# Hybrid decoder block: the first norm from squares of the transposed input, row blocks of the second product group prepared one ahead, and modulation rows summed by fp32r products

## The chip, the cores and the metric

The kernel runs on one NeuronCore of one Trainium2 chip. The metric is the device time of one execution in microseconds (us). The engines are named as in the profile: PE (TensorE, the matrix products; its weight loads are PEld), DVE (VectorE), ACT (ScalarE), POOL (GpSimd) and SP (SyncE, which only issues transfers here). Each runs its own instructions in order and waits on the others by semaphores.

## The reference, cut to what matters

The block takes x (1024 tokens by 1024 channels, float32), a conditioning vector c and weights. What the change touches is the beginning, and the rows of the modulation that are needed later:

```
silu_c = silu(c)
mod = silu_c @ w_ada + b_ada              # 6 * 1024 columns
shift1, scale1, gate1, shift2, scale2, gate2 = split(mod, 6)
h = rms_norm(x, norm1_w) * (1 + scale1) + shift1
proj = h @ w_in                           # v, q, k, a_lr, sv, r, g_a, su, g_b ...
...                                       # gated linear attention, spatial gating, merge, w_out
x = x + gate1 * y
h2 = rms_norm(x, norm2_w) * (1 + scale2) + shift2
...                                       # PEER: top-16 of 16384 experts for 8 heads, gathers
x = x + gate2 * y2
out = rms_norm(x, final_norm_w)
```

rms_norm divides each token by the root of the mean of its squared channels (plus 1e-6).

## The kernel before

**Precision.** A float32 product is split: an operand is rounded to fp32r (its high part, written by ACT), DVE subtracts that from the operand (its low part, also fp32r), and three fp32r products stand for one. In the first group the even row blocks of weights are multiplied whole, in plain fp32, and only the odd ones are split.

**Halves.** The tokens are worked in two halves of 512. For the first half the first two groups of products (the two halves of the columns of v, `w_inp[G_V0]` and `w_inp[G_V1]`) are written out by hand in `first_groups`, because the modulation, the norm and the weights arrive at the same time as they are needed. Every instruction there goes through `put`, which chains it behind the instruction before it on its engine, so that the order in the source is the order on each engine. (The profile shows all of these at line 1088, the line of `put`; they are told apart by their tiles.) After that the order is the planner's, within the edges that `issue_after` gives.

**First group, rounds q = 0 to 3.** The contraction runs over 8 row blocks k of 128 channels. `xts[k]` is x transposed, 128 channels by 512 tokens; `wts[k]` is a row block of weights. Round q handles the blocks ka = 2q (by `whole`: 4 fp32 products) and kb = 2q+1 (by `products`: 12 fp32r products into the same 4 PSUM banks `mm`), and meanwhile forms the scale columns of the next round: `channel_sums` multiplies 8 row blocks of `w_ada` by silu(c) and adds them up (`add`: the first on ACT, the others on DVE, tile `adc`), `close` sums over the partitions by products with a column of ones on PE (tile `aux`), and `store_scale` writes `mod` and `scol` on DVE. The next round's `scaled` on ACT multiplies `xts` by `scol`, in place, and needs that. The first group is computed without the norm, and its result is scaled by `rstd` per token when it leaves PSUM (`evac0`, tile `vt`). The shift is added much later (`shift_rows`, `shift_sum`, `shift_add`).

**The norm.** x itself, tokens on partitions, is read into four tiles `xb` (512 KB each). ACT squares each and sums along the row (`squares(0)` in round 2, `squares(2)` in round 3). `norm` scales the four sums on DVE and takes the power -0.5 on POOL; `norm_spread` writes `dg`, a diagonal matrix of rstd, on DVE; `norm_rows` multiplies it by ones on PE and copies the result to `rrow` on ACT. In round 3 the order on PE is: 4 whole products of block 6, `norm_rows`, the 12 products of block 7, `close` for the shift columns.

**Second group, k = 0 to 7.** Here the normed and shifted input is needed: `turn(k)` (DVE) multiplies `xts[k]` by `rrow` (and by `scol` for odd k), `split_h(k)` writes `hTh` (ACT) and `hTl` (DVE), `high` and `low` split the weights (`wh` on ACT, `wl` on DVE), then come 12 products and two small ones for the decay rank (`alpha`). In each step k everything of block k stands just before its products. DVE also sums the second half of the shift columns, two rows in each of the steps 0 to 3; `close` stands inside step 3, and `store_shift(nps, 1)` after it. After the group come `decay(0)` and `decay(1)`, and `shift_rows` may start behind the group's last DVE instruction (`hlast[1]`).

**Modulation rows.** The other four parts of the modulation are made during later groups of the first half, by `ada_row`: DVE sums 8 tiles of 128 by 1024 (tile `adacc`), and two fp32 products with a column of ones, each giving 1 by 512, sum over the partitions (line 1174).

**Pools.** `v4` has 4 buffers of 128 by 1024, `b4` has 8, `aux` has 2 PSUM banks.

Of the kernel before, what the change touches and what calls it, by code (L numbers as in the profile page):

```python
# [80 lines left out]
def block_kernel(ctx: ExitStack, tc: tile.TileContext, x, xT, cT, w_asc, w_ash, w_ada, b_ada, b_adaT, n1T, w_inp, w_alr,  # L81
# [27 lines left out]
    nc.vector.tensor_scalar(ident, jp, 0.0, None, op0=OP.is_equal)  # L109
    nc.vector.tensor_scalar(ltri, jp, 0.0, None, op0=OP.is_gt)  # L110
    nc.vector.memset(ones, 1.0)
    nc.vector.memset(mhalf, -0.5)
    for i in range(5):
        nc.vector.memset(bit5[:, i:i + 1], 1 << i)
# [905 lines left out]
    class Queue:  # L1020
# [4 lines left out]
        def add(self, g):  # L1025
            self.gens.append(g)
# [27 lines left out]
    with ExitStack() as pa:  # L1054
# [109 lines left out]
        def ada_row(c, r):  # L1164
            for acc in ada_acc(c):
                yield
            for _ in range(2):
                yield
            row_ = t4("adarow")
            nc.scalar.dma_start(row_[0:1], b_ada[:, c * D:(c + 1) * D])  # L1170
            for n in range(2):
                sl = slice(n * 512, (n + 1) * 512)
                ps = auxt([1, 512])
                nc.tensor.matmul(ps, ones[:, 0:1], acc[:, sl], start=True, stop=True)
                nc.vector.tensor_tensor(row_[0:1, sl], row_[0:1, sl], ps, op=OP.add)
            if r == 1:
                nrow = t4("nrow")
                nc.scalar.dma_start(nrow[0:1], n2_w)
                nc.vector.scalar_tensor_tensor(row_[0:1], row_[0:1], 1.0, nrow[0:1], op0=OP.add, op1=OP.mult)
            nc.scalar.dma_start(rows_d[r:r + 1, :], row_[0:1])  # L1180
            yield
# [28 lines left out]
                    xts.append(xt[:, kk])  # L1210
            return xts

        hlast = []

        def h_split(k):
            xt = xts[k]
# [7 lines left out]
        def first_groups(evac0, evac1, aps, finish_alpha, decay):  # L1224
# [97 lines left out]
            by_bank = [(n, i) for i in range(4) for n in range(3)]  # L1322

            rrow = t2("rrow")
            ss = sm_p.tile([P, BH], F32, name="ss")

            def squares(i0):
                for i in (i0, i0 + 1):
                    put("scalar", "activation", xb[i], xb[i], AF.Square, accum_out=ss[:, i:i + 1])

            def norm():
                rstd = sm_p.tile([P, BH], F32, name="rstd")
                rstd0.append(rstd)
                put("vector", "tensor_scalar", rstd, ss, 1.0 / D, EPS, op0=OP.mult, op1=OP.add)
                nc.gpsimd.tensor_tensor(rstd, rstd, mhalf[:, :BH], op=OP.pow)
# [24 lines left out]
            ps, prod, add, close = channel_sums(scs[0], [0, 1, 2, 3], 2 * P)  # L1360
            prod([0, 1, 2, 3])
            add(KD)
            close()
            store_scale(ps, 0)
            keep_warm(iota)
# [3 lines left out]
            scaled(hTh[:, 1], 1)  # L1369
            wl = low(wts[1], wh)  # L1370
            scaled_low(1)
            xb, shs = [], []
            for q in range(4):
                ka, kb = 2 * q, 2 * q + 1
                nps, _, add, close = channel_sums(scs[q + 1], [], 2 * P) if q < 3 else channel_sums(shs[0], [], 512)
                whole(pss, ka)
                if q == 3:
                    squares(2)
                add(1)
                if q < 3:  # L1380
                    nwh = high(wts[kb + 2])
                    if q == 2:
                        squares(0)
                    add(KD)
                    if q:
                        scaled_low(kb)
                    nwl = low(wts[kb + 2], nwh)
                else:
                    add(2)
                    norm()  # L1390
                    scaled_low(kb)
                    add(2)
                    norm_rows(norm_spread())
                    add(KD)
                cut = (8, 4, 4, 12)[q]
                order = by_bank if q == 3 else by_part
                products(pss, kb, wh, wl, order[:cut])
                close()
                products(pss, kb, wh, wl, order[cut:])
                if q == 0:  # L1400
                    scs.append(load_scale(3, b4))
                    load_x(6, 7)
                    load_w(6, 7)
                    for i in range(BH):
                        xb.append(v4.tile([P, D], F32, name="xb", tag="v4"))
                        put("sync", "dma_start", xb[i], x[i * P:(i + 1) * P, :])
                    put("sync", "dma_start", walr, w_alr)
                    load_w1(0)
                    shs.append(load_shift(0))
                    load_w1(1, 2)  # L1410
                if q == 2:
                    shs.append(load_shift(1))
                    load_w1(3, 4)
                    for dst, src_ in ((wal[:RANK], w_al), (wal[RANK:], w_al), (balt, b_alT), (keyst, keysT), (sgub, sgu_bT)):
                        put("sync", "dma_start", dst, src_)
                if q < 3:
                    store_scale(nps, q + 1)
                    scaled(xts[kb + 1], kb + 1)
                    scaled(hTh[:, kb + 2], kb + 2)
                    wh, wl = nwh, nwl  # L1420
                else:
                    for i in range(4):
                        evac0(i, pss[i])
                    turn(0)
                    nwh = high(w1[0])
                    store_shift(nps, 0)
                    nwl = low(w1[0], nwh)
            split_const(walr, walr2[:, :, :RANK], walr2[:, :, RANK:])
            keep0.extend(wts)
            nps, _, add, close = channel_sums(shs[1], [], 512)  # L1430
            pss1 = [mm.tile([P, 512], F32, name="mm", tag="mm") for _ in range(4)]
            for k in range(KD):
                if k:
                    turn(k)
                    nwh = high(w1[k])
                split_h(k)
                if k:
                    nwl = low(w1[k], nwh)
                if k + 5 < KD:
                    load_w1(k + 5)  # L1440
                if k == KD - 1:
                    alpha(aps, k, put)
                if k < 4:
                    add(2)
                order = by_bank if k in (0, KD - 1) else by_part
                products(pss1, k, nwh, nwl, order[:8])
                if k == 3:
                    close()
                products(pss1, k, nwh, nwl, order[8:])
                if k < KD - 1:  # L1450
                    alpha(aps, k, put)
                if k == 3:
                    store_shift(nps, 1)
                    split_const(wal, wal_h, wal_l)
# [3 lines left out]
                evac1(i, pss1[i])  # L1458
            decay(0)
            decay(1)  # L1460
            return tail["tensor"]

        S = []
# [39 lines left out]
        for hf in range(NHALF):  # L1503
# [70 lines left out]
            def shift_rows(k0):  # L1574
                if not shiftw:
                    shiftw.append(rp.tile([P, 512], F32, name="so", tag="so", bufs=2))
                for k in (k0, k0 + 1):
                    if k == 0:
                        with tc.issue_after(hlast[1]):
                            nc.vector.tensor_scalar(shiftw[0], keep0[0], mod[:, 0:1], None, op0=OP.mult)  # L1580
                    else:
                        nc.vector.scalar_tensor_tensor(shiftw[0], keep0[k], mod[:, k:k + 1], shiftw[0], op0=OP.mult, op1=OP.add)
# [496 lines left out]
```

## Time and profile before

| | |
|---|---|
| times of 3 runs | 1439.87, 1431.17, 1432.71 us; median 1432.71 |
| profiled execution, its own time | 1431.43 us |
| its span, first to last instruction | 1429.6 us (1.8 us lie around it) |
| PE busy | 1338.7 us, 94% of the span |
| DVE busy | 1085.0 us, 76% |
| ACT busy | 694.2 us, 49% |
| POOL busy | 291.5 us, 20% |
| DMA | 341.90 MB moved |
| mean granted PE clock | 0.972 |

The busy shares are means over the whole span. All but the four modulation rows of what the change touches lies in the first 92 us, and those rows lie between 187 and 284 us.

### The profile page before, as it was taken

How to read it: one execution, taken by the hardware profiler on the slowest of the kernel's cores; microseconds unless marked ns; L12 is line 12 of the kernel's file. 1: busy time of each engine (PE TensorE's matmuls, PEld its weight loads, DVE VectorE, ACT ScalarE, POOL GpSimd, SP SyncE). 2: the span in 40 equal slices, each digit the busy share in tenths (PEclk: the TensorE clock that was granted, in tenths of full speed). 3: DMA queues.
4: the chain of work that ended last, by engine and by line, in shares of the span. 5: the costliest groups of instructions: out<-in, count | busy, mean ns of one | idle time of the engine just before them, and what ended most of it. 6: DMA issues, size and time to landing. Idle time of an engine off the chain costs nothing. (4 is left out here: it accounts for less than half of the span.)

```text
span 1429.6 us, 19379 instructions
## 1 busy us (share of the span) xinstructions
PE 1338.7 (94%) x5952; PEld 1027.3 (72%) x5952; DVE 1085.0 (76%) x3094; ACT 694.2 (49%) x1561; POOL 291.5 (20%) x270
## 2 busy tenths in 40 slices
PE   9799999999999999988989999999998999789994
PEld 5578867788888887776867888877777876345552
DVE  5685569834468678999789887888798767898783
ACT  4364342333345465475344565655455545555542
POOL 0020001000000122341441142311111124453320
PEclk9899999999999999998999999999998999999997
DMA  9344446732257475777687799987687559998972
GB/s 361 131 155 134 137 152 203 252 97 83 94 177 264 160 276 176 274 236 243 205 285 255 244 357 333 332 305 243 234 294 284 197 171 382 349 386 340 369 292 104
DMA packets 111877, 341.90 MB, mean 239 GB/s; under 512 B 14505, under 2 KB 15785, under 8 KB 99602
## 3 DMA queue, kind: packets, MB, share of 16 engines
q0 software_dynamic: 31344, 163.85, 31.4%
q1 hardware_dynamic: 63072, 131.37, 27.0%
q10 hardware_dynamic: 17346, 45.34, 8.9%
q8 instruction: 48, 0.79, 0.2%
q14 instruction: 67, 0.55, 0.1%
HBM read 316.28 MB, written 24.23 MB: 238 GB/s over the span
## 5 line engine op out<-in xcount | busy, mean ns | idle before, releaser
L1497 ACT ACTIVATE wh<-wt 128x512 fp32r<-128x512 f32 x336 | 207.8, 627 | 280.8 <-PE mm L183 116.2
L1499 DVE TENSOR_TENSOR wl<-wt,wh 128x512 fp32r<-128x512 f32 x336 | 227.2, 689 | 109.2 <-ACT wh L1497 58.1
L182 PE MATMUL mm<-wh,hTh 128*128 128x512 f32 x624 | 246.0, 394 | 2.1 <-ACT wh L1497 2.1
L183 PE MATMUL mm<-wh,hTl 128*128 128x512 f32 x624 | 245.7, 394 | 0.0
L185 PE MATMUL mm<-wl,hTh 128*128 128x512 f32 x624 | 194.5, 395 | 2.2 <-DVE wl L1499 2.2
L182 PEld LDWEIGHTS mm<-wh,hTh 128*128 128x128 f32 x624 | 117.4, 188 | 28.8 <-ACT wh L1497 3.1
L185 PEld LDWEIGHTS mm<-wl,hTh 128*128 128x128 f32 x624 | 116.0, 188 | 29.6 <-DVE wl L1499 3.0
L526 POOL DMA_INDIRECT uv<-in_tab_dram,ix x74 | 80.6, 1089 | 274.7 <-ACT ix L558 170.9
L183 PEld LDWEIGHTS mm<-wh,hTl 128*128 128x128 f32 x624 | 117.2, 188 | 25.1 <-issue 0.9
L182 PE MATMUL mm<-hTh,wh 128*128 128x512 f32 x240 | 96.0, 400 | 0.0
L581 DVE SCALAR_TENSOR_TENSOR uv<-uv,hps 128x512 f32<-128x512 f32 x112 | 75.1, 684 | 26.7 <-DMA uv<-in_tab_dram,ix 16.0
L183 PE MATMUL mm<-hTl,wh 128*128 128x512 f32 x240 | 95.0, 396 | 0.0
L188 PE MATMUL mm<-wh,hTh 128*128 128x512 f32 x208 | 84.0, 410 | 4.7 <-DVE x L1886 2.1
L190 PE MATMUL mm<-wh,hTl 128*128 128x512 f32 x208 | 81.8, 393 | 0.0
L189 PE MATMUL mm<-wl,hTh 128*128 128x512 f32 x208 | 81.7, 393 | 0.0
L188 PE MATMUL mm<-hTh,wh 128*128 128x256 f32 (+1 forms) x208 | 71.2, 345 | 8.9 <-DVE q L1673 6.6
L185 PE MATMUL mm<-hTh,wl 128*128 128x512 f32 x240 | 72.3, 401 | 0.0
L189 PE MATMUL mm<-hTl,wh 128*128 128x256 f32 (+1 forms) x208 | 69.3, 335 | 3.1 <-DVE hTl L174 3.1
L753 POOL DMA_INDIRECT uvd<-in_down_dram,dix x32 | 38.2, 1193 | 163.9 <-DVE ts L360 47.2
L190 PE MATMUL mm<-hTh,wl 128*128 128x256 f32 (+1 forms) x208 | 68.2, 336 | 0.0
L619 DVE SCALAR_TENSOR_TENSOR vl<-uv,r,vh 128x512 fp32r<-128x512 f32 x82 | 59.6, 749 | 9.3 <-ACT vh L618 5.8
L607 PE MATMUL acc<-uv,W 128*128 128x512 f32 x132 | 63.4, 603 | 2.5 <-ACT W L596 1.9
(970 smaller groups left out, 2955.7 us busy)
## 6 DMA issues: line engine op xcount, KB each, us to landing
wt<-in_w_inp_dram SPq DMA_DIRECT2D x216, 256.0 KB
wt<-in_w_qp_dram SPq DMA_DIRECT2D x72, 256.0 KB
wada<-in_w_ada_dram SPq DMA_DIRECT2D x32, 512.0 KB
wt<-in_w_outp_dram SPq DMA_DIRECT2D x56, 256.0 KB
s_d<-so ACTq DMA_DIRECT2D x28, 256.0 KB
wada<-in_w_asc_dram SPq DMA_DIRECT2D x8, 512.0 KB
xb<-in_x_dram SPq DMA_DIRECT2D x8, 512.0 KB
wada<-in_w_ash_dram SPq DMA_DIRECT2D x8, 512.0 KB
```

Of the source, the lines that this page charges most:

```text
L182: nc.tensor.matmul(ps, lh, rh, start=False, stop=False)
L183: nc.tensor.matmul(ps, *((lh, rl) if feat else (ll, rh)), start=False, stop=False)
L185: nc.tensor.matmul(ps, *((ll, rh) if feat else (lh, rl)), start=False, stop=False)
L188: nc.tensor.matmul(ps, lh, rh, start=first, stop=False)
L189: nc.tensor.matmul(ps, lh, rl, start=False, stop=False)
L190: return nc.tensor.matmul(ps, ll, rh, start=False, stop=last).ins
L526: nc.gpsimd.indirect_dma_start(out=dst[:], out_offset=None, in_=src, in_offset=off)
L581: nc.vector.scalar_tensor_tensor(uv[0][:, sl], uv[0][:, sl], 1.0, hps, op0=OP.mult, op1=OP.mult, accum_out=r[:, 2 + n:3 + n])
L607: ins = nc.tensor.matmul(acc[:, sl], W, v[:, sl], start=first, stop=last).ins
L619: nc.vector.scalar_tensor_tensor(vl, v, r[:, 5:6], vh.bitcast(F32), op0=OP.mult, op1=OP.subtract)
L1497: nc.scalar.activation(wh, wt, AF.Identity)
L1499: nc.vector.tensor_tensor(wl, wt, wh.bitcast(F32), op=OP.subtract)
```

## The change

1. The norm of the first half comes from `xts`, the transposed x that is loaded anyway. In each round ACT squares two blocks of `xts` (before `scaled` overwrites them) into a tile `sq` of 128 by 1024, DVE adds the tiles up (`add_squares`), and in round 3 DVE adds the two halves and four products with a column of ones give the sum of squares per token (`sum_squares`). The four tiles `xb` and their loads (2 MB) go; the loads of the shift weights move up into their place, and those of `walr` behind them.
2. In the second group the work of block k+1 (`turn`, `high`, `low`) is issued in step k, before the products of step k. The additions for the shift columns are spread 3, 2, 2 over the steps 0 to 2, and the eighth row is summed by 4 direct products on PE in step 1.
3. `ada_row` rounds its sum to fp32r on ACT, takes the rest on DVE, and sums both by fp32r products (4 of them in place of 2 in fp32). Two tiles of `b4` are added for each row.
4. `shift_rows` may start only behind the DVE instructions of `decay(1)`.

```
+    oner = const.tile([P, 1], F32R, name="oner")
+    nc.vector.tensor_copy(oner, ones[:, 0:1])
...
         def ada_row(c, r):
             for acc in ada_acc(c):
                 yield
-            for _ in range(2):
-                yield
+            yield
+            ah = b4.tile([P, D], F32R, name="adah", tag="b4")
+            al = b4.tile([P, D], F32R, name="adal", tag="b4")
+            nc.scalar.activation(ah, acc, AF.Identity)
+            nc.vector.tensor_tensor(al, acc, ah.bitcast(F32), op=OP.subtract)
+            yield
...
-                nc.tensor.matmul(ps, ones[:, 0:1], acc[:, sl], start=True, stop=True)
+                nc.tensor.matmul(ps, oner, ah[:, sl], start=True, stop=False)
+                nc.tensor.matmul(ps, oner, al[:, sl], start=False, stop=True)
...
-            def squares(i0):
-                for i in (i0, i0 + 1):
-                    put("scalar", "activation", xb[i], xb[i], AF.Square, accum_out=ss[:, i:i + 1])
+            def squares(q):
+                sq = v4.tile([P, D], F32, name="sq", tag="v4")
+                for n in range(2):
+                    put("scalar", "activation", sq[:, n * HALF:(n + 1) * HALF], xts[2 * q + n], AF.Square)
+                sqs.append(sq)
+            def add_squares():
+                put("vector", "tensor_tensor", sqs[0], sqs[0], sqs[-1], op=OP.add)
+            def sum_squares():
+                put("vector", "tensor_tensor", sqs[0][:, :HALF], sqs[0][:, :HALF], sqs[0][:, HALF:], op=OP.add)
+                ss = auxt([P, BH])
+                for i in range(BH):
+                    put("tensor", "matmul", ss[:, i:i + 1], sqs[0][:, i * P:(i + 1) * P], ones[:, 0:1], ...)
+                return ss
...
             add(KD)
+            squares(0)
             close()
...
             for q in range(4):
                 ...
+                if q == 3:
+                    ss = sum_squares()
                 whole(pss, ka)
-                if q == 3:
-                    squares(2)
                 add(1)
                 if q < 3:
                     nwh = high(wts[kb + 2])
-                    if q == 2:
-                        squares(0)
+                    squares(q + 1)
                     add(KD)
                     if q:
                         scaled_low(kb)
                     nwl = low(wts[kb + 2], nwh)
+                    add_squares()
                 else:
-                    add(2)
-                    norm()
+                    add(1)
+                    norm(ss)
+                    add(1)
                     scaled_low(kb)
                     add(2)
                     norm_rows(norm_spread())
                     add(KD)
...
-                    for i in range(BH):
-                        xb.append(v4.tile([P, D], F32, name="xb", tag="v4"))
-                        put("sync", "dma_start", xb[i], x[i * P:(i + 1) * P, :])
+                    shs.append(load_shift(0))
+                    load_w1(0)
                     put("sync", "dma_start", walr, w_alr)
-                    load_w1(0)
-                    shs.append(load_shift(0))
                     load_w1(1, 2)
...
-            nps, _, add, close = channel_sums(shs[1], [], 512)
+            nps, prod, add, close = channel_sums(shs[1], [KD - 1], 512)
             for k in range(KD):
-                if k:
-                    turn(k)
-                    nwh = high(w1[k])
+                wh, wl = nwh, nwl
                 split_h(k)
-                if k:
-                    nwl = low(w1[k], nwh)
                 ...
-                if k < 4:
-                    add(2)
+                if k + 1 < KD:
+                    turn(k + 1)
+                    nwh = high(w1[k + 1])
+                if k < 3:
+                    add((3, 2, 2)[k])
+                if k + 1 < KD:
+                    nwl = low(w1[k + 1], nwh)
-                products(pss1, k, nwh, nwl, order[:8])
+                products(pss1, k, wh, wl, order[:8])
+                if k == 1:
+                    prod([KD - 1])
                 if k == 3:
                     close()
-                products(pss1, k, nwh, nwl, order[8:])
+                products(pss1, k, wh, wl, order[8:])
...
             decay(1)
+            decayed.append(tail["vector"])
...
-                        with tc.issue_after(hlast[1]):
+                        with tc.issue_after(decayed[0]):
                             nc.vector.tensor_scalar(shiftw[0], keep0[0], mod[:, 0:1], None, op0=OP.mult)
```

## Rows read from the trace of the kernel before

**Rows 1.** The page: busy time of each engine, its share of the span and the number of instructions.

```profile
PE 1338.7 (94%) x5952; PEld 1027.3 (72%) x5952; DVE 1085.0 (76%) x3094; ACT 694.2 (49%) x1561; POOL 291.5 (20%) x270
```

**Rows 2.** The waits of the first 95 us: who waited, and for whom; us in total, how often, the longest.

```profile
PE aux L1088 <- DVE dg L1088: 4.3, 1, 4.3
...
PE mm L1088 <- ACT hTh L1088: 2.3, 2, 1.2
```

**Rows 3.** The timeline of PE from the first group's second round to the start of the second group. Columns: start us, length us, engine, line, operation, output<-inputs, shape, count, and in brackets the idle time before it and who ended it. An fp32 product shows as two records.

```profile
17.30 1.18 PE L1088 MATMUL mm<-wh,hTl 128*128 128x512 f32 x4
18.87 3.70 PE L1088 MATMUL mm<-w,xt 128*128 128x512 f32 x8 [0.40 <-ACT xt L1088]
...
26.00 3.60 PE L1088 MATMUL mm<-w,xt 128*128 128x512 f32 x8
...
32.92 3.60 PE L1088 MATMUL mm<-wst,xt 128*128 128x512 f32 x8
40.83 2.05 PE L1088 MATMUL aux<-dg,ones 128*128 128x512 f32 x2 [4.32 <-DVE dg L1088]
41.89 1.42 PE L1088 MATMUL mm<-wh,hTh 128*128 128x512 f32 x1
...
47.26 0.95 PE L1088 MATMUL aux<-ones,adc 128*128 128x1 f32 x8
49.39 0.50 PE L1088 MATMUL mm<-wh,hTh 128*128 128x512 f32 x1 [1.18 <-ACT hTh L1088]
...
50.63 0.79 PE L1088 MATMUL mm<-wh,hTl 128*128 128x512 f32 x1 [0.51 <-DVE hTl L1088]
```

**Rows 4.** Windows of 3.41 us, cut where the granted clock changes. Columns: the window, its length, busy time and instruction count of PE, PEld, DVE, ACT and POOL, the granted PE clock, the DMA share, GB/s.

```profile
39.77:43.18 3.41, 2.35 (x4) 1.25 (x5) 3.08 (x5) 0.26 (x1) 0.00 (x0) 0.50 1.00 389
...
46.60:50.01 3.41, 2.23 (x14) 1.69 (x12) 1.38 (x5) 3.18 (x6) 0.00 (x0) 1.00 0.02 6
50.01:53.42 3.41, 2.90 (x8) 2.21 (x8) 2.62 (x5) 1.70 (x3) 0.00 (x0) 0.50 0.23 77
53.42:56.84 3.42, 3.42 (x10) 2.30 (x9) 2.64 (x5) 0.71 (x2) 0.00 (x0) 0.50 0.22 77
67.08:70.49 3.41, 2.13 (x8) 1.47 (x9) 2.30 (x4) 1.53 (x3) 0.00 (x0) 1.00 0.03 5
```

**Rows 5.** The timeline of ACT in the first rounds, and one square of the norm.

```profile
16.44 0.63 ACT L1088 ACTIVATE wh<-w 128x512 fp32r<-128x512 f32 x1 [3.41 <-DMA w<-in_w_inp_dram]
18.10 0.72 ACT L1088 ACTIVATE xt<-xt,scol 128x512 f32<-128x512 f32 x1 [1.02 <-DVE scol L1088]
...
19.34 0.49 ACT L1088 ACTIVATE adc<-wada,sc 128x256 f32<-128x256 f32 x1
21.66 0.63 ACT L1088 ACTIVATE wh<-w 128x512 fp32r<-128x512 f32 x1 [1.82 <-DMA w<-in_w_inp_dram]
...
34.26 1.04 ACT L1088 ACTIVATE xb<-xb 128x1024 f32<-128x1024 f32 x1
```

**Rows 6.** The timeline of DVE in the first rounds and before the norm's product.

```profile
19.86 3.61 DVE L1088 SCALAR_TENSOR_TENSOR adc<-wada,sc,adc 128x256 f32<-128x256 f32 x7 [1.80 <-ACT adc L1088]
23.39 0.75 DVE L1088 SCALAR_TENSOR_TENSOR hTl<-xt,scol,hTh 128x512 fp32r<-128x512 f32 x1
24.05 0.69 DVE L1088 TENSOR_TENSOR wl<-w,wh 128x512 fp32r<-128x512 f32 x1
24.65 0.15 DVE L1088 TENSOR_TENSOR mod<-aux,badat 128x2 f32<-128x2 f32 x1
...
38.55 1.53 DVE L1088 SCALAR_TENSOR_TENSOR adc<-wada,sc,adc 128x512 f32<-128x512 f32 x2
40.00 0.68 DVE L1088 TENSOR_TENSOR dg<-ident,rstd 128x512 f32<-128x512 f32 x1
```

**Rows 7.** Instructions by line, shapes kept apart: a DVE sum of two tiles of 128 by 1024, and the power on POOL in the first 120 us. Columns: line, engine, operation, tiles, shapes, count, busy us, mean ns of one, idle us before.

```profile
L1901 DVE TENSOR_TENSOR xr<-xr,sh 128x1024 f32<-128x1024 f32 x8 | 9.7, 1220 | 0.0
...
L1335 POOL TENSOR_TENSOR rstd<-rstd,mhalf 128x4 f32<-128x4 f32 x1 | 1.4, 1447 | 35.4 <-DVE rstd L1088 35.4
```

**Rows 8.** The timeline of PE in the second group and at its end, and the direct products of the first round.

```profile
5.75 1.95 PE L1088 MATMUL aux<-sc,wada 128*128 128x1 f32 x16
...
68.17 1.20 PE L1088 MATMUL mm<-wh,hTh 128*128 128x512 f32 x4 [1.16 <-ACT hTh L1088]
...
71.97 1.09 PE L1088 MATMUL mm<-wh,hTh 128*128 128x512 f32 x4
...
75.18 1.07 PE L1088 MATMUL mm<-wh,hTh 128*128 128x512 f32 x4
...
81.62 0.50 PE L1088 MATMUL gaux<-alh,wal_h 32*128 32x512 f32 x1
```

**Rows 9.** The timeline of PE at the third modulation row: its two fp32 sums and the product after them.

```profile
258.19 1.88 PE L1174 MATMUL aux<-adacc,ones 128*1 128x512 f32 x4
260.00 0.50 PE L188 MATMUL mm<-wh,hTh 128*128 128x512 f32 x1
```

**Rows 10.** Windows around the modulation rows, columns as in rows 4.

```profile
220.00:240.00 20.00, 18.56 (x77) 13.46 (x77) 20.00 (x30) 5.44 (x9) 4.10 (x3) 1.00 0.62 198
...
260.00:283.87 23.87, 23.87 (x101) 18.19 (x100) 18.68 (x25) 7.23 (x12) 0.00 (x0) 1.00 0.68 236
```

**Rows 11.** The waits of PE from 85 to 640 us: who waited for whom; us in total, how often, the longest.

```profile
PE mm L185 <- DVE wl L1499: 2.2, 2, 1.3
```

More of the change, by code (lines that the diff above doesn't have):

```diff
@@ L1211, in x_prep @@
             return xts
-        hlast = []
+        hlast, decayed = [], []
         def h_split(k):
@@ L1324, in first_groups, with norm @@
             rrow = t2("rrow")
-            ss = sm_p.tile([P, BH], F32, name="ss")
-            def squares(i0):
-                for i in (i0, i0 + 1):
-                    put("scalar", "activation", xb[i], xb[i], AF.Square, accum_out=ss[:, i:i + 1])
-            def norm():
+            sqs = []
+            def squares(q):
[9 more added lines that the diff above has]
+                for i in range(BH):
+                    put("tensor", "matmul", ss[:, i:i + 1], sqs[0][:, i * P:(i + 1) * P], ones[:, 0:1], start=i == 0,
+                        stop=i == BH - 1)
+                return ss
+            def norm(ss):
                 rstd = sm_p.tile([P, BH], F32, name="rstd")
@@ L1371, in first_groups @@
             scaled_low(1)
-            xb, shs = [], []
+            shs = []
             for q in range(4):
```

## The prediction

> **What bounds the kernel now.** I began with the busy times of the page: PE has 94% of the span [rows 1], so the question for each edit is what it does to PE's stream. Outside the modulation rows everything touched is over by 92 us, so I then took PE's waits of the first 95 us [rows 2]: the longest is 4.3 us, the norm's product waiting for `dg`; 2.3 us go to waits for `hTh` in the second group. PE's timeline puts them in order [rows 3]. From 18.87 on the rounds run without a gap (18.87, 26.00, 32.92: 7.13 and 6.92 us each); then comes the 4.32 us hole before 40.83. The price of the hole is more than its length: the granted clock is 0.50 in the window that begins at 39.77 [rows 4], and the 12 products of block 7 take 5.4 us (41.89 to 47.26), 0.43 to 0.45 each. Between 47.26 and 50.63 only the tiny sums, a wait of 1.18 us, two products and a wait of 0.51 us stand, and the clock is 0.50 again from 50.01 to 56.84 [rows 4]. So two clock drops and about 7.5 us of waits are what there is to win at the head.
>
> The profiled execution took 1431.43 us, its span 1429.6; my sum is made on that. The median of the three runs, 1432.71, lies 1.3 us above it.
>
> **The rounds get longer.** A round's loop runs through ACT and DVE [rows 5, 6]: `xt` at 18.10, `adc` at 19.34, ready 19.83, seven additions from 19.86 to 23.39, `hTl` 0.66, `wl` 0.60, `mod` at 24.65, and the next `xt` about 0.38 later (25.03): 6.93 us, just under PE's 7.13. The change puts one sum of 128 by 1024 into that loop ahead of `mod`: 1.22 us [rows 7]. The loop becomes 8.15 us and DVE sets the round. The squares on ACT are not shown with this shape; a square of 128 by 1024 without the row sum took 1.04 [rows 5], so I take 0.52 each (from 0.5, half of that, to 0.7, the scaled copy `xt`). In rounds 2 and 3 they lie in ACT's wait for `scol` and cost nothing; without it 1.04 more each.
>
> In round 1 they do cost. `wh` waits for its transfer until 16.44 [rows 5] in either kernel; the squares follow it, to 18.2. DVE's sum must wait for them, ends at 19.4, and the next `xt` starts at 19.7 instead of 18.10. PE's second round starts 0.77 after `xt`, at 20.5 (+1.6, a hole of 2.0). Round 3: `xt` at 27.85, PE at 28.6 (+2.6, hole 1.0). Round 4: `xt` at 36.0. PE, however, has the sums of squares ahead of its whole products: half addition 0.6 on DVE, four tiny products 0.5 (16 of the same form took 1.95 [rows 8]), so PE starts at 37.1 (+4.2). `squares(0)` before round 1 fits ACT's wait before its first `xt` or delays it by up to 0.6; I take 0.
>
> **The norm gets out of the way.** Now `dg` hangs on DVE's order alone: `adc` on ACT from 37.25 to 37.95, then on DVE an addition 0.67, rstd 0.1, an addition 0.67, `hTl` 0.66, two additions 1.45 (38.55 to 40.00 [rows 6]), `dg` 0.68: 42.1 to 42.2. POOL's 1.45 us [rows 7] run beside these. PE ends the whole products at 37.1 + 3.6 = 40.7 and waits 1.4, not 4.3. So the norm's product starts 1.3 later than before (40.83). With PE at full clock it takes 0.9 (a whole product: 3.60 for four [rows 3]), the 12 products 12 x 0.227 = 2.7 (four take 0.91 where PE is unhindered: 75.18 - 71.97 = 3.21 for 12 and two small ones [rows 8]); they end at 45.8, not 47.26. The path from there to the second group (`close`, evacuation, `wh`, `hTh`) stays 49.39 - 47.26 = 2.13: the second group starts at 47.9, 1.5 us sooner. Transfers don't bind here: the shift weights take the place of 2 MB of x, and move up.
>
> **The second group.** Before: 49.39 to 81.62, 32.2 us. After: eight steps of 3.21 = 25.7, `close` 0.8, direct products of row 8 0.5, and in step 0 a wait for `hTl(0)`, 0.7 (0.51 before; nothing is ahead of it yet): 27.7. DVE needs 0.67 + 0.67 + 0.61 + 1.34 = 3.3 per step while it adds, no more than PE's step, and one step of lead hides the rest. The hole of 1.16 at 68.17 [rows 8] goes, because `turn(4)` no longer queues behind `store_shift` and the wait for `close`; what comes late next is `hTh(4)`, some 1.2 after `close`, inside the 1.4 of products still queued. The clock: from 45.8 to 49.1 PE is nearly empty, so I expect one more drop, near 50; as PE is then busy without a break, it lasts one window of 3.41 (the second window before came after one with the break at 50.1), which costs half, 1.7. End: 47.9 + 27.7 + 1.7 = 77.3, against 81.62: **4.3 us sooner**. `shift_rows` behind `decay(1)` costs nothing: its eight DVE instructions (8 x 0.67 = 5.4) are needed by `shift_sum`, five steps into the next group (5 x 12 x 0.227 = 13.6 of PE); were that cover gone, up to 5.4 would show.
>
> **The clock rule of the skill.** The trace drops the clock after a window with PE 65% busy by its records, many of them one column wide (46.60), and not after one with 62% of full products (67.08) [rows 4]. The Trainium skill, page "TensorE: Matmul & The Clock Gate", section "Part 1: The HAM clock gate (the "warmup" mystery)", asks for an idle window of about 3.4 us before the clock drops. By that the new head, whose longest whole hole is 2.0, would never drop; the trace speaks against it, and I keep it as a rival below.
>
> **The modulation rows.** Two fp32 sums hold PE for 260.00 - 258.19 = 1.81 [rows 9]; four fp32r ones would take 4 x 0.227 = 0.91. That is 0.9 per row, 3.6 for four, where PE is full (23.87 of 23.87 [rows 10]). Against it stands 1.22 on DVE per row (ACT has room). The second row falls between 220 and 240, where DVE is busy 20.00 of 20.00 and PE is not [rows 10]; there PE's gain is worth nothing and the 1.22 is on the path. So -2.7 + 1.2 = **-1.5**; ends: -3.6, if it hides everywhere, and +1.3 (4 x 1.22 - 3.6), if nowhere. Two more `b4` buffers per row can hold up the next row's loads on SP, with weight loads behind them; the old row held its sum just as long, until its product, so I price this at 0, upper end in +1.3.
>
> **Sum.** 1431.4 - 4.3 - 1.5 = 1425.6. PE's few waits from 85 to 640 us come from engines that move along with it (the one on DVE adds to 2.2 us [rows 11]), so I carry the lead to the end.
>
> **The rivals.** *The clock never drops* in these groups: 1.7 more, 1423.9; with the rows' full 3.6, 1421.8. For it: no whole hole is near 3.4 us. Against: the drop at 50.01. *DVE becomes the bound, and the kernel gets slower.* Place: the three sums in the rounds and one per modulation row. If the holes at 18.5, 27.6, 35.5 and 40.7 add up to an empty window, the clock is down at 42.1 as it was at 40.83, and the rounds' loss is not won back: +1.3 at the second group; that group takes 27.7 and two cold windows 3.4, ending 0.1 late; rows +1.3: 1432.8. It decides once a window around 36 to 42 falls under about half busy; I make it 55 to 60%. Against: just that margin. *The lead is absorbed later*, by gathers or by another order of the planner, which is free after `first_groups`: 1431. For it: the planner sees other times. Against: PE is nearly full to 640 us.
>
> **How the numbers follow.** Forecast 0.45; clock never drops 0.20; DVE bound 0.15; absorbed 0.15; 0.05 for another order that is worth more than all this, either way. The forecast's own range is 1423.5 (rows hide everywhere) to 1428.4 (nowhere). The whole range runs from 1420, the second case with the rows' full gain and a couple of us of other order, to 1434, the third case and the 1.3 by which the median lies above. Faster by over 1% (under 1418, about what a measurement of this kernel can tell from no change is 1%) needs 13 us, twice what I find: 0.06. Slower by over 1%: 0.02.
>
> **What would show it.** The start of PE's second, third and fourth round (+1.6, +2.6, +4.2), with DVE as releaser; `dg` at about 42.1; a clock of 1.00 at the norm's product; the second group from 47.9 to 77.3 without the hole in step 4; 0.9 instead of 1.8 at the rows. I am wrong if the clock is down through the first group, if the rounds stay near 7 us, or if the lead at 82 us is not there at the end.

## The result and the profile after

| | before | after |
|---|---|---|
| median, runs shown side by side | 1433.26 us (7 runs, 1430.93 to 1439.87) | 1421.82 us (7 runs, 1417.08 to 1428.10) |
| ratio | | 0.9917 [0.9889, 0.9944] |
| profiled execution, its own time | 1431.43 us | 1428.10 us |
| its span | 1429.6 us | 1426.4 us |

The time lies in the range (1420 to 1434), 3.8 us below the forecast of 1425.6, and within 1% of before, as I gave 0.92 to. As a difference it is less tidy: 11.4 us between the medians, where my sum had 5.8; the interval of the ratio is 8 to 16 us. A profiled execution is a single draw, from 8.0 us below the median of its kernel (no_rows) to 9.5 us above it (sum_late), and that of the changed kernel is the slowest of its set here and again in after_again, a second set of runs below that gave the same gain; so its traces show how the stages went, but not the whole of the gain.

The page of after, for [rows 1]:

```profile
PE 1337.2 (94%) x5968; PEld 1033.6 (72%) x5968; DVE 1093.0 (77%) x3102; ACT 699.2 (49%) x1565; POOL 294.5 (21%) x270
```

PE did 1.5 us less, DVE 8.0 more. The lines are shifted by the added ones: `put` is now L1090. The waits of the first 95 us, for [rows 2]:

```profile
PE mm L1090 <- ACT xt L1090: 1.5, 3, 0.9
PE aux L1090 <- DVE dg L1090: 1.2, 1, 1.2
PE mm L1090 <- ACT hTh L1090: 1.1, 1, 1.1
...
PE aux L1090 <- DVE sq L1090: 0.7, 1, 0.7
```

The 4.3 us for `dg` have become 1.2, the 2.3 for `hTh` 1.1; the waits for `xt` in the rounds have grown from 0.7 to 1.5, and one for `sq` is new. PE's timeline puts them in order, for [rows 3, 8]; each line starts with its start and length:

```profile
20.22 3.70 PE L1090 MATMUL mm<-w,xt 128*128 128x512 f32 x8 [0.43 <-ACT xt L1090]
...
28.35 3.70 PE L1090 MATMUL mm<-w,xt 128*128 128x512 f32 x8 [0.86 <-ACT xt L1090]
...
36.37 1.02 PE L1090 MATMUL aux<-ones,sq 128*128 128x1 f32 x8 [0.72 <-DVE sq L1090]
37.25 3.68 PE L1090 MATMUL mm<-wst,xt 128*128 128x512 f32 x8
42.09 1.10 PE L1090 MATMUL aux<-dg,ones 128*128 128x512 f32 x2 [1.16 <-DVE dg L1090]
...
45.76 0.95 PE L1090 MATMUL aux<-ones,adc 128*128 128x1 f32 x8
47.83 0.53 PE L1090 MATMUL mm<-wh,hTh 128*128 128x512 f32 x1 [1.12 <-ACT hTh L1090]
...
49.07 0.80 PE L1090 MATMUL mm<-wh,hTl 128*128 128x512 f32 x1 [0.29 <-DVE hTl L1090]
...
77.53 0.49 PE L1090 MATMUL gaux<-alh,wal_h 32*128 32x512 f32 x1
```

I had written 20.5, 28.6 and 37.1 for the rounds, 42.1 for the norm's product, 45.8 for the end of its 12 products, 47.9 for the second group and 77.3 for its end. The windows of the clock, columns as in [rows 4]:

```profile
44.75:48.17 3.42, 2.30 (x16) 1.98 (x14) 1.14 (x5) 3.37 (x6) 0.00 (x0) 1.00 0.01 2
48.17:51.58 3.41, 3.12 (x8) 2.05 (x7) 3.38 (x6) 1.99 (x4) 0.00 (x0) 0.50 0.23 77
...
102.77:106.18 3.41, 1.42 (x6) 0.88 (x6) 3.41 (x8) 0.35 (x1) 0.00 (x0) 1.00 0.26 79
106.18:109.60 3.42, 3.42 (x10) 2.63 (x9) 3.42 (x9) 2.47 (x5) 0.00 (x0) 0.50 0.22 74
```

One half-clock window in the head, as priced, and one at 106.18 that was not in the sum.

For the comparison of whole traces I matched PE's instructions by their tiles and took the median shift against the kernel before at a few places. Minus is earlier; us, one profiled execution each:

| place in before, us | 85 | 140 | 320 | 480 | 525 | 740 | end |
|---|---|---|---|---|---|---|---|
| after | -4.1 | -1.4 | -3.6 | -3.0 | +1.5 | -2.6 | -3.2 |
| after_again | -4.5 | -1.8 | -4.2 | -3.3 | +2.1 | +0.5 | -4.4 |

So the head is worth what I said at 85 us; 2.7 us go at once between 85 and 140; the rows bring 1.4 to 1.6 from 190 to 320; and 4.5 to 5.4 us go near 500 us. By these traces alone a gain of 3 to 4 us was to be expected, and the medians show three times that. The experiments ask where each of these steps comes from.

### The profile page after: what moved, and what is told of

The parts are those of the page before. It is cut to its first block, busy times and chain, and to the rows that moved or that the text cites. A ratio compares the mean times of both kernels' runs of the same rounds, so it can differ in the third digit from the quotient of the medians.

```text
span 1426.4 us, 19428 instructions
## 1 busy us (share of the span) xinstructions
PE 1337.2 (94%) x5968; PEld 1033.6 (72%) x5968; DVE 1093.0 (77%) x3102; ACT 699.2 (49%) x1565; POOL 294.5 (21%) x270
## 4 chain that ended last, share of the span: by engine, by line
PE 41%; DVE 10%; DMA 8%; ACT 3%; issue 3%; POOL 1%; ACTq 0%; DVEq 0%; SPq 0%; POOLq 0%
PE mm L184 6%; PE mm L185 6%; PE mm L187 6%; PE acc L609 6%; PE mm L190 3%; PE mm L191 3%; PE mm L192 3%; DMA uv<-in_tab_dram,dix 3%; PE hps L581 1%; PE aux L1988 1%; PE hps L582 1%; PE acc L629 1%; PE acc L628 1%; DMA uvd<-in_down_dram,dix 1%; DVE uv L583 1%
## 5 line engine op out<-in xcount | busy, mean ns | idle before, releaser
L528 POOL DMA_INDIRECT uv<-in_tab_dram,ix x74 | 83.6, 1130 | 258.7 <-ACT ix L560 135.6
```

Of the source, the lines that this page charges most:

```text
L528: nc.gpsimd.indirect_dma_start(out=dst[:], out_offset=None, in_=src, in_offset=off)
```

## The experiments

All ratios are against runs of the kernel before on the same chip (their medians were 1431.05, 1433.45, 1436.06 and 1435.30 us in the four sets); 0.1% is 1.4 us. The ratios are not the quotients of the medians; for no_rows that quotient is 0.9996.

**after_again**: the changed kernel, unedited.

> The changed kernel once more, unedited, for a second profile and times beside the runs that follow. My theory: 4.1 us at the head, seen again at the end of the second group (77.5 against 81.6), and the rest of the 11 us between the medians lies in the modulation rows and in clock drops that fall differently from run to run; time about 1422, and a second profile in which the lead of 4.1 at 78 us is the same but the lead at 520 us is not. Rival: what the first profile loses behind the head (2.7 us near 105, 4.5 near 500) belongs to the changed order and comes again at the same places.

Measured: 1419.58 us, 0.9909 [0.9883, 0.9934]. The gain is 11 to 13 us, twice my sum. The loss after 85 us and that near 500 come again, so of the two expectations it was the rival that came. after_one, below, loses 4.7 us near 500 too; no_gate, whose order from 140 us on is the same, does not, so this loss does not come in every trace.

**no_rows**, **only_norm** and **only_ahead**: the parts.

```
no_rows      the changed kernel, ada_row as before
only_norm    the kernel before + part 1
only_ahead   the kernel before + part 2
```

> The changed kernel with the modulation rows summed in fp32 as before. My theory: rows are worth 1.5 (1.3 lost to 3.6 won), so 1423 to 1425. Rival, that the rows (or the order that the planner makes around them) carry what the head does not explain: 1428 to 1429. The head ends at 77.5 in both.

> The kernel before with the norm from squares of the transposed x alone; second group and rows as before. My theory: the norm's product at about 42.1 at full clock, the second group at 47.8, then the old second group of 32 us (hole in step 4, one or two half-clock windows): ends near 79.5 to 80, 1.5 to 2 us sooner than before, 1431 to 1432. Rival, that the rounds' three sums on VectorE cost what the norm wins: same as before, 1433, or later.

> The kernel before with the second group's blocks prepared one ahead alone. My theory: start of the second group stays at 49.4; the hole of 1.2 in step 4 goes, 0.5 comes for the direct products, and one half-clock window instead of two saves 1.7: ends near 79.2, 2.4 us sooner, 1431. Rival, that the parts work only together because the clock is down either way at 50 us: 0.7 sooner, 1432.6.

Measured: no_rows 1430.44, 0.9977 [0.9956, 0.9998]; only_norm 1419.78, 0.9919 [0.9890, 0.9948]; only_ahead 1426.98, 0.9963 [0.9935, 0.9991]. One part alone brings as much as all, and all but the rows brings almost nothing, so the parts do not add up. Yet their leads at 480 us are much alike (1.9 us for the norm, 1.6 for the second group, 1.8 for no_rows, which has both and the gate). Compared instruction by instruction, each of these kernels has another order on PE, DVE and ACT from about 600 to 1300 us than the kernel before, where no line was edited: the planner sees slightly other times. no_rows and only_ahead have nearly the same late order, the changed kernel another, and only_norm one that no other run has. That became the second theory: the order of the late stages is worth several us.

**after_one**: the changed kernel with one product more, whose result nobody reads, which is enough to give it the late order of no_rows.

```
+            keep_warm(iota)
             hlast[:] = [tail["scalar"], tail["vector"]]
```

> The changed kernel with one more product of 128x256 (ones by the iota tile, result unused) at the end of the second group, near 77 us. It costs PE at most about 0.5 us. The planner's model of time moves by that much, and it arranges what follows 600 us differently: from there on the order on PE and DVE is that of the kernel that had everything of the change but the rows (no_rows, 1430.4), not that of the changed kernel (1419.6 to 1421.8). Theory 'late order': the head is worth only 3 to 4 us and the order after 600 us the rest, so this goes to about 1427 to 1430. Theory 'carried lead': the head decides, 1420 to 1422.

Measured: 1418.88, 0.9916 [0.9888, 0.9943]. As I had put it, the second theory falls: the order of no_rows is as good as that of the changed kernel. What was left of it is that the order of the kernel before is the slow one.

**before_six**, **before_five** and **before_eleven**: the kernel before with a few idle ACT instructions of 128 by 8 at the end of the second group.

```
+            for _ in range(6):     # 5, 11
+                put("scalar", "activation", sc, sc, AF.Identity)
             hlast[:] = [tail["scalar"], tail["vector"]]
```

> The kernel before with six more ACT instructions of 128x8 (on a tile no longer needed) at the end of the second group, some 1.2 us on ACT near 81 us. Nothing else is changed in the source; with five of them the planner's order stays that of the kernel before, with six it takes from 600 us on the order of no_rows. Theory 'late order': the time may move by some us though the head is the same or up to 1 us later; by only_ahead (same order, 1427.0 with a lead of 1.6 at 480 us) about 1428 to 1429. Theory 'carried lead': 1431 to 1432.

> The kernel before with five ACT instructions of 128x8 at the end of the second group instead of six. The planner's order on every engine from 850 us on is that of the kernel before (28 small shifts ahead of it). It is the control of before_six (1428.7, ratio 0.9969), whose order after 600 us differs at 575 places. If the order after 600 us is what gave before_six its 4 to 5 us, this is as the kernel before: ratio 0.999 to 1.001. If it was something about the added instructions or the stretch from 60 to 220 us, which the two share, the ratio is 0.996 to 0.998.

> The kernel before with eleven such ACT instructions (about 2 us of ACT near 80 us). With this number the order on PE from about 630 us on, and on DVE and ACT, is that of the changed kernel, while the head is that of the kernel before or up to 1 us later. If the order is worth what the head's lead does not explain (the changed kernel is 11.5 to 12 faster with a lead of 3 to 4 at 320 us): 1424 to 1426, ratio 0.993 to 0.996. If the order does not matter: ratio 0.999 to 1.001.

Measured: before_five 1434.03, 0.9989 [0.9965, 1.0014]; before_six 1428.68, 0.9969 [0.9942, 0.9996]; before_eleven 1429.51, 0.9961 [0.9942, 0.9981]. Five keep the old order from 850 us on and change nothing that can be measured; six and eleven, with other late orders (six that of no_rows, eleven that of the changed kernel), are 4.4 and 5.6 us faster, though their heads are no better (all three lead by 1.2 to 1.3 us at 85 us, and before_eleven is 1.7 late at 320). The interval of the five overlaps with those of the other two, so I go by both of them being on one side, and by the trace. In the trace, PE's waits from 600 to 740 us: before,

```profile
PE mm L188 <- DVE q L1673: 5.8, 1, 5.8
PE gaux L1716 <- DVE rdr L768: 5.2, 1, 5.2
PE aux L278 <- DVE cnt L275: 1.6, 1, 1.6
PE mm L188 <- ACT vt L1564: 1.3, 1, 1.3
```

and before_eleven, in its stretch 603.2 to 738.2:

```profile
PE mm L188 <- DVE q L1675: 4.8, 1, 4.8
PE gaux L1718 <- DVE rdr L768: 4.5, 1, 4.5
PE gaux L1719 <- DVE S L1720: 0.6, 1, 0.6
PE gaux L1707 <- ACT ot L1721: 0.2, 1, 0.2
```

The wait for `cnt` is gone. It is a product of one column for the routing of the experts. In the old order PE is ready for it at 674.7, while DVE works on two `kk` first and has `cnt` only at 676.2; in the new one DVE is done before PE comes to it (PE's timeline, before and then before_eleven):

```profile
676.28 0.38 PE L278 MATMUL aux<-cnt,ltri 128*128 128x1 f32 x2 [1.59 <-DVE cnt L275]
676.52 1.46 PE L1714 MATMUL aux<-vt,ktok 128*128 128x256 f32 x4
```

```profile
676.62 0.28 PE L278 MATMUL aux<-cnt,ltri 128*128 128x1 f32 x2
676.76 1.30 PE L1716 MATMUL aux<-vt,ktok 128*128 128x256 f32 x4
```

This wait is in the traces of the three kernels with the old order (before, before_five, head_old_order) and in none of the other eleven. From 655 to 690 us the eleven gain 2.4 to 2.8 us on the kernel before, before_five 1.4, head_old_order nothing; in before and in head_old_order a half-clock window follows the wait (at 678.06 in before, after a window with PE 1.73 us busy of 3.41).

A second place is a product that waits for DVE's `x`, the sum with the residual behind `w_out` (PE's timeline, before and then before_eleven):

```profile
1037.21 0.50 PE L188 MATMUL mm<-wh,hTh 128*128 128x512 f32 x1 [2.13 <-DVE x L1886]
```

```profile
1032.62 0.39 PE L188 MATMUL mm<-wh,hTh 128*128 128x512 f32 x1
```

The three with the old order wait 2.1, 2.9 and 0.3 us here (before, before_five, head_old_order), and in the eleven no such product waits for `x`; from 1000 to 1060 us the eleven gain 2.1 to 5.2 us on the kernel before, head_old_order 1.7, before_five nothing. From 525 to 1330 us the three take 805.0, 803.2 and 802.2 us of PE's stream, the others 787.5 to 801.8 but for one (sum_late, 805.5). So by before_six and before_eleven the old order costs about 4 to 6 us, and these two places are the larger part of it, as far as one trace of each kernel can tell.

**head_old_order**: the counterpart. The changed kernel without the rows, and with one product as in after_one; the planner then gives it, from 180 us on, exactly the order of the kernel before.

> The changed kernel without its third part (the modulation rows stay fp32) and with one more product of 128x256 at the end of the second group. With it the planner's order from 165 us on is, on PE, DVE and ACT, exactly that of the kernel before, so only the head is changed: its lead is about 4 us at 85 us and 1.5 to 3 from 140 to 480 (no_rows has 4.2, then 1.6). If the lead is carried and the order after 600 us is worth what before_six and before_eleven show, the ratio is 0.997 to 0.999, and the rest of the change's gain belongs to that order and to the rows. If the order does not matter and the head is what gains: 0.991 to 0.993. If the lead is taken back on the way (by the transfers near 500 us): 0.999 to 1.001.

Measured: 1428.46, 0.9963 [0.9942, 0.9985]; its lead is 4.8 at 85 us, 2.7 at 320 and 4.4 at the end. On the way, at 1000 us, none of it is left against the trace of before. Against before_five, which has the old late order too, it is steadier: 3.6 at 85 us, 2.4 at 320, 4.7 at 525, 4.6 at 1000 and 5.7 at the end. So the head's lead is carried to the end, with about its own size (5.3 us by the ratio, 2.1 to 8.3 by the interval). One thing speaks against the price of the order: no_rows differs from this kernel by that one product and the late order alone, and with the other order it is not faster (0.9977 against 0.9963, on another chip).

**no_gate**: the changed kernel without part 4.

```
-                        with tc.issue_after(decayed[0]):
+                        with tc.issue_after(hlast[1]):
```

> The changed kernel without its fourth part: shift_rows may start behind hlast again, as before, not behind decay(1). From 140 us on its order is the changed kernel's. I priced the gate at 0. If the loss of 2.7 us near 105 us in the changed kernel (DVE's q 2.0 us late instead of 0.8, then a window at half clock) comes from the gate, the lead at 120 us is 3 to 4 us here (1.4 to 1.75 with the gate) and, carried, the time 1418 to 1420. If the loss belongs to something else, the lead at 120 stays at 1.5 to 2 and the time at 1420 to 1422; if the gate is a gain, 1 to 4 us more.

Measured: 1419.19, 0.9911 [0.9885, 0.9937]. The loss near 105 us is the gate's: from 85 to 140 us the changed kernel loses 2.7 us of its lead, and without the gate it gains 0.6. sum_late and late_nogate, below, differ by the gate alone too, and lose 2.8 and gain 0.5. PE's waits from 85 to 140 us, after and then no_gate:

```profile
PE mm L190 <- DVE q L1696: 2.0, 1, 2.0
```

```profile
PE mm L190 <- DVE q L1696: 0.2, 1, 0.2
```

and on DVE the additions of the shift to `vt`, again after and then no_gate:

```profile
102.00 2.47 DVE L1618 TENSOR_TENSOR vt<-vt,aux 128x512 f32<-128x512 f32 x4
...
105.00 0.41 DVE L1695 SCALAR_TENSOR_TENSOR qs<-mm,eG 128x256 f32<-128x256 f32 x1
105.33 0.40 DVE L1696 SCALAR_TENSOR_TENSOR q<-mm,eG 128x256 f32<-128x256 f32 x1
```

```profile
98.99 2.48 DVE L1618 TENSOR_TENSOR vt<-vt,aux 128x512 f32<-128x512 f32 x4
...
102.32 0.42 DVE L1696 SCALAR_TENSOR_TENSOR q<-mm,eG 128x256 f32<-128x256 f32 x1
```

With the gate the eight rows end later, `shift_sum` and these four additions with them, and they meet the evacuation of `q` that PE waits for; a half-clock window follows (106.18 above). That window is not sure: after_one, no_rows and head_old_order have the gate and waits of 1.5, 2.0 and 1.4 us, but no half-clock window there, and lose only 0.6 to 1.2 us. Without the gate the lead at 320 us is 7.7 instead of 3.6 to 4.2, but the time at the end is not measurably better.

**sum_late** and **late_nogate**: the sum of the squares moved behind the scale columns; late_nogate also without the gate.

```
                     nwl = low(wts[kb + 2], nwh)
-                    add_squares()
...
                     store_scale(nps, q + 1)
+                    add_squares()
```

> The changed kernel with DVE's sum of the squares (128x1024, 1.22 us) put behind the scale columns of the next round (mod, scol) instead of ahead of them; its order after 800 us is that of the changed kernel. The rounds on PE should go back to about 7 us (starts near 18.9, 26, 33 instead of 20.2, 28.4, 37.3), the norm's product to about 38 to 39, and the lead at 80 us should grow by 3 to 4 us. If a lead at the head is carried to the end: about 1417. If something later takes it back (the gathers, a wait on a transfer): 1420 to 1422 as the changed kernel.

> The changed kernel with DVE's sum of the squares behind the scale columns (as in sum_late) and without the gate on shift_rows (as in no_gate); from 810 us on it has the changed kernel's order. The lead at 80 us should be that of sum_late, 7 to 8 us, and the loss of 2.7 us near 105 us should not come. If a lead at the head is carried: 3 to 4 us below no_gate (ratio 0.9911), a ratio of 0.988 to 0.989. If the transfers of the second half's x near 500 us take it back (in the changed kernel the last of them lands at 505.5 as before, though it was issued 3 us sooner): as no_gate and the changed kernel, 0.990 to 0.992.

Measured: sum_late 1423.87, 0.9931 [0.9906, 0.9956]; late_nogate 1424.53, 0.9926 [0.9904, 0.9949]. The head does what was expected (PE's timeline of sum_late):

```profile
19.64 3.70 PE L1090 MATMUL mm<-w,xt 128*128 128x512 f32 x8 [0.23 <-ACT xt L1090]
...
26.75 3.60 PE L1090 MATMUL mm<-w,xt 128*128 128x512 f32 x8
...
39.54 1.10 PE L1090 MATMUL aux<-dg,ones 128*128 128x512 f32 x2 [0.19 <-DVE dg L1090]
...
45.29 0.49 PE L1090 MATMUL mm<-wh,hTh 128*128 128x512 f32 x1 [1.12 <-ACT hTh L1090]
```

The round is 7.1 us again, the clock does not drop in the head, and both kernels lead by 7.8 us at 85 us, 3.5 more than the changed kernel. Neither is faster at the end than the changed kernel: the expectation of 1417 failed. Part of the way back can be read. From 190 to 320 us PE waits more for `sg` (the gate of the spatial part, on DVE, which is full from 220 to 240 us [rows 10]); after, and then late_nogate:

```profile
PE mm L190 <- DVE sg L1805: 3.1, 2, 1.8
```

```profile
PE mm L190 <- DVE sg L1805: 4.3, 2, 3.6
```

The other part is near 500 us, where the lead of the changed kernel goes too. There ACT squares four tiles of the second half's x as they land, and `qt`, which PE waits for, stands behind them on ACT. ACT's timeline and PE's, before:

```profile
505.57 1.06 ACT L1201 ACTIVATE xb<-xb 128x1024 f32<-128x1024 f32 x1 [1.39 <-DMA xb<-in_x_dram]
...
507.14 1.55 ACT L1916 ACTIVATE qt<-mm 128x512 f32<-128x512 f32 x3
```

```profile
507.77 0.71 PE L1965 MATMUL aux<-keyst,qt 128*128 128x128 f32 x4 [1.08 <-ACT qt L1916]
```

and after:

```profile
505.48 1.06 ACT L1208 ACTIVATE xb<-xb 128x1024 f32<-128x1024 f32 x1 [1.45 <-DMA xb<-in_x_dram]
...
507.06 1.55 ACT L1939 ACTIVATE qt<-mm 128x512 f32<-128x512 f32 x3
```

```profile
507.69 0.71 PE L1988 MATMUL aux<-keyst,qt 128*128 128x128 f32 x4 [4.02 <-ACT qt L1939]
```

The transfers were issued 3 us sooner in the changed kernel (SP's timeline, before and after), and the last tile is there at the same time:

```profile
494.54 1.85 SPq L1200 DMA_DIRECT2D xb<-in_x_dram  x4
```

```profile
491.50 2.17 SPq L1207 DMA_DIRECT2D xb<-in_x_dram  x4
```

They share the DMA engines with weights and with the first gathers, and their busy share is 1.01 to 1.04 from 500 to 508 us in both. PE comes 3 us sooner and waits 3 us longer, and then has a half-clock window. In no_gate the same wait is 1.4 us and the lead stays: there the four transfers were issued 7.1 us sooner than in the kernel before, and the last square starts 6.8 us sooner. From issue to that square it is 11.0 us in before, 14.0 in after and 11.3 in no_gate; what makes it 14.0 no run here shows. So this seam can take a lead of 3 us whole, or none of it; which of the two a median run does, the traces cannot say, being one execution each.

## Why the prediction was right, and where it was not

**The head: right, nearly term by term.** PE's second, third and fourth rounds came 1.35, 2.35 and 4.3 us later (1.6, 2.6 and 4.2 forecast), with ACT's `xt` and DVE's sum behind them; the sums of squares cost 1.22 and 0.68 us on DVE, the squares on ACT 1.13 to 1.15 for two (1.04 taken). `dg` made the norm's product start at 42.09 (42.1), at full clock; the second group went from 47.83 to 77.53 (47.9 to 77.3), without the hole in step 4 and with one half-clock window. The lead there is 4.1 and 4.5 us in two executions (4.3). Two terms came from a misread row: the 16 records of [rows 8] are eight fp32 products, so four of them were to be priced at 0.98, not 0.5. The four that sum the squares took 0.88 (36.37 to 37.25), the four direct ones of row 8 took 0.81. It hardly shows, because `xt` came at 35.71 and not at 36.0, and the wait for `hTl(0)` was 0.29 and not 0.7; that is luck.

**The clock: right as the trace of before had it, with luck in the count.** The head dropped once, after a window with no empty stretch over 1.2 us; near 105 it dropped after one with PE 1.42 of 3.41 us busy. sum_late had none after a window with the same busy time as the one at 44.75, but with 9 records, none of them one column wide, in place of 16, of which eight are:

```profile
44.69:48.10 3.41, 2.30 (x9) 1.61 (x10) 3.34 (x7) 2.61 (x5) 0.00 (x0) 1.00 0.23 77
```

no_gate has the changed kernel's head on PE, to 0.15 us up to the start of the second group, and no drop in it; its windows lie otherwise:

```profile
44.07:47.48 3.41, 2.54 (x16) 2.16 (x14) 1.13 (x3) 3.34 (x6) 0.00 (x0) 1.00 0.01 2
47.48:50.89 3.41, 2.65 (x10) 1.92 (x11) 3.34 (x7) 2.58 (x5) 0.00 (x0) 1.00 0.24 77
```

So the one drop that I priced hangs on where the windows fall.

The Trainium skill, page "TensorE: Matmul & The Clock Gate", section "Part 1: The HAM clock gate (the "warmup" mystery)", wants an idle window for the drop. After an empty window the drop does come (before, 1241.26 to 1244.67, PE 0.00 us busy), but behind the windows of 44.75 and 102.77, with PE 2.30 and 1.42 us busy, it came without one. That the windows run freely, at fixed steps of 3413 ns, as the same section says, does agree: 48.17 and 106.18 are 17 such steps apart. The busy time alone does not settle it either: the clock dropped after 2.10 of 3.41 us (after, 1000.49 to 1003.90) and not after 1.44 (no_rows, 718.71 to 722.12).

**The rows: right on the sum, by luck.** Four fp32r products take 0.93 (267.65 to 268.58 at one row) where the two fp32 ones took 1.81 [rows 9] (PE's timeline, one row, two of its four and what follows):

```profile
189.37 0.40 PE L1180 MATMUL aux<-adah,oner 128*1 128x512 f32 x1
189.60 0.40 PE L1181 MATMUL aux<-adal,oner 128*1 128x512 f32 x1
189.84 0.39 PE L184 MATMUL mm<-wh,hTh 128*128 128x512 f32 x1
```

and the rest on DVE costs 1220 ns. From 190 to 320 us the lead grows by 1.4 and 1.6 us (1.5). But no_rows and head_old_order, which have this head without the rows, lose 1.6 and 1.5 us of their lead there. Against them the rows are worth about 3 us in this stretch, nearer to the 3.6 for rows that hide everywhere; half of that makes up for lead that is lost. What the rows are worth at the end is not settled: after_one and no_rows have one late order and differ by the rows and one product, and lie 0.61% apart (on two chips), some 9 us, far more than any price of mine.

**The gate: wrong, 0 taken.** I said that the eight instructions have 13.6 us until `shift_sum` needs them. I priced the step by who needs the result and not by what follows it on DVE: the four additions to `vt` moved 3 us and met `q`. I had also taken all but the rows to be over by 92 us; these additions run from 102.0 to 104.5. It costs 1.8 us of wait and, in both traces of the changed kernel, a half-clock window of 1.7, inside the 5.4 that I named for the case without cover, but it did not enter my sum.

**"I carry the lead to the end": right on the whole, but not for the reason given.** head_old_order bears it out for a lead of this size. But PE is not as full as I took it to be from 85 to 640 us: leads of 3 us and more are taken back at `sg` and, in some executions, at the second half's x, which did not arrive sooner there. The rival "absorbed later" names this; what it takes from the median of the changed kernel no run shows, but by their traces it is what sum_late and late_nogate ran into.

**The order of the planner: the term that was missing.** I had 0.05 for "another order that is worth more than all this, either way". It came: 4.4 to 5.6 us (before_six, before_eleven), beside 5.3 for the head in the old order (head_old_order). Together 9.7 to 10.9, with 1.5 for the rows 11.2 to 12.4; the change was measured at 11 to 13. Another way to the same place: before_eleven has the changed kernel's late order without the change, and the change lies 6.3 to 7.5 us below it by the ratios (of which up to 1.7 may be before_eleven's own, being that late at 320 us). So the forecast of 5.8 was about right for what the change does in its own place, as far as intervals of 3 to 4 us either way can tell. That the time came out in the range is luck: other terms had made the range wide, and the median of the second set, 1419.58, lies just below it.

The sum does not close for two kernels. no_rows has the head and another order and should be near 0.993; it measured 0.9977, with an interval that begins at 0.9956. only_norm has a lead of 2 us and another order and should be near 0.995; it measured 0.9919, with an interval that ends at 0.9948. That stays open, and so the sum is an account, not a proof: that the order is worth several us rests on before_six and before_eleven, and not on every pair.

## What to carry to other kernels

Where a planner orders the work from modelled times, an edit at the head moves the order far behind it; before a gain of some us is put down to an edit, give the kernel before a neutral edit that changes the order, and the changed kernel one that gives it the old order back. A lead is worth what the tightest later wait on another engine or on a transfer leaves of it: past that, more lead at the head buys nothing. A step that is held back is to be priced by what stands behind it on its engine, not only by who needs its result.

## What the runs showed of the hardware

Two things that I had not expected. In these traces a window in which PE has little full work is often followed by one at half clock, and the windows lie on a fixed grid, so the same hole costs 1.7 us or nothing by where it lies: after has a half-clock window at 48.17, and no_gate, with the same head, has none. And an earlier issue is not always an earlier arrival: four loads of 512 KB that were issued 3.0 us sooner, with a DMA share of 1.01 to 1.04 from 500 to 508 us, let their last square start only 0.1 us sooner in after, while in no_gate 7.1 us brought 6.8.
